# Down projection on unscaled products, with the gate applied at the end and three quadrants added into the output by accumulating DMA

## The chip, the cores and the metric

The kernel runs on one core of a Trainium2 chip. The metric is the device time of one execution in microseconds, as the median of several runs. The core's engines work side by side, each through its own list of instructions in a fixed order: TensorE (PE; its weight loads are listed as PEld), VectorE (DVE), ScalarE (ACT), GpSimd (POOL), and SyncE (SP), which here issues DMA transfers.

## The reference

One block of a diffusion transformer on 1024 tokens of width 1024 (`x`), with 256 context tokens. Only the first layer of the reference is run (`DEPTH = 1`). Cut to what matters:

```python
sh1, sc1, g1, sh2, sc2, g2 = adaln(c, w_mod, b_mod)          # six rows of 1024
h = modulate(rms_norm(x, norm1), sh1, sc1)                   # and the same for the context
y = neighbourhood_attention(q, k, v, kc, vc, rpb) @ w_o      # 16 heads
x = x + g1 * y                                               # called x1 below
h = modulate(rms_norm(x, norm2), sh2, sc2)
a, g = split(h @ w_up, 2)                                    # 2 x 2816 columns
x = x + g2 * ((a * gelu(dwconv_centred(g, conv_w, conv_b))) @ w_down)
```

The last line is the feed-forward part. `g2` is one value for each of the 1024 output columns; `w_down` is 2816 x 1024. Everything is float32.

## The kernel before, in words

Tokens are held in 8 tiles of 128 (`t` = 0 to 7). Every product is taken with operands split into a high part (`h`, a rounded copy made by ScalarE) and a low part (`l`, the rest, a subtraction by VectorE or GpSimd), as three matmuls: high by high, high by low, low by high.

The stages, in the order of the program text: adaLN of the attention branch, attention with the query/key/value projections in between, output projection, second norm (`h2_tile`), up projection with convolution and gate, down projection. The text is only an order of preference: a planner with a cost model of its own lays each engine's instructions out by when it expects them to be ready, preferring those that come earlier in the text. On the chip each engine then keeps to the order laid out, so that an instruction that waits holds up all that stand behind it on its engine. Stages overlap in this way; parts of the down projection stand between parts of the up projection.

`h2_tile(t)` (L621) stores the finished tile of x1 in a scratch tensor `x1_dram`, normalises it and writes the modulated, transposed result over the tile.

The up and the down projection both use a form with seven products of half-size blocks in place of eight. For the down projection the gated rows, and sums of them, were written to `act_dram` by the up projection's `finish`: seven blocks for each of 11 chunks of 256 rows of `w_down`. The chunks are worked in groups of 2, 3, 3 and 3 (`GROUPS`, L45), and in each group the seven products in the order 2, 1, 5, 6, 3, 7, 4 (`DORD`, L58). `seq` lists the 28 pairs (group, product); for each pair there are three steps:

- `prep_b` (L874): on the first pair, and at product 6 of the group before, `load_raw` (L853) fetches the rows of `w_down` as tiles `dr` of 128 x 1024 and multiplies each by `g2b`, the row `g2` on all partitions (L862: of a chunk's two tiles one on GpSimd, the other on VectorE). Products 5, 6, 7 and 4 first form a difference of blocks in place on VectorE (L887 to L893). Then ScalarE makes the high part (L895) and VectorE (products 2, 1, 7) or GpSimd (5, 6, 3, 4) the low part, tile `db` (L896).
- `prep_a` (L865): loads the block of `act_dram` into `da`, and splits it the same way (L869 to L871).
- `down_mm` (L899): for each of four column tiles `j`, nine matmuls (six in the first group) into one of two sets of four PSUM banks, `X` (products 1, 6, 7, 4) and `Y` (2, 5, 3), which go on accumulating over products; then VectorE adds the bank to a half of an accumulator tile `acc[t]` (L914). Each product belongs to one quadrant (row half of the tokens, column half of the outputs): 2 and 1 to (0, 0), 6 and 3 to (0, 1), 5 and 7 to (1, 1), 4 to (1, 0).

`prep_b` runs two pairs ahead of `down_mm`, `prep_a` three. There are 12 buffers for `da` and 10 for `db`. The accumulators are loaded with x1 from `x1_dram` before the first pair (L924), and in the last group, after a quadrant's last product (1, 3, 7, 4), its four tiles are stored to the output by SP (L916). All DMA transfers are issued by SP.

Of the kernel before, what the change touches and what calls it, by code (L numbers as in the profile page):

```python
# [10 lines left out]
F32 = mybir.dt.float32  # L11
F32R = mybir.dt.float32r
AF = mybir.ActivationFunctionType
ALU = mybir.AluOpType
# [4 lines left out]
P = 128  # L19
# [5 lines left out]
NB = 8  # L25
# [11 lines left out]
HALF = 512  # L37
# [7 lines left out]
GROUPS = [2, 3, 3, 3]  # L45
# [8 lines left out]
DG = (1,)  # L54
# [3 lines left out]
DORD = (2, 1, 5, 6, 3, 7, 4)  # L58
# [3 lines left out]
def block_kernel(ctx, tc, x, ctxt, cc, w_mod, b_col, b_row, n1, n2, w_qkv, gains, rpb_t, mask_i, mask_r, w_o,  # L62
                 w_up, conv_w, conv_b, w_down, comb, out):
    nc = tc.nc
    PE, ACT, DVE, POOL, SP = nc.tensor, nc.scalar, nc.vector, nc.gpsimd, nc.sync

    def pool(name, bufs=1, space=None, side=None):
        kw = {}
        if space is not None:
            kw["space"] = space  # L70
        if side is not None:
            kw["side"] = side
        if space is not DRAM:
            kw["reuse_waits"] = "tile"
        return tc.tile_pool(name=name, bufs=bufs, **kw)

    def f(ap):
        return ap.bitcast(F32)

    xv = x.rearrange("(r b j) d -> b r j d", r=ROWS, b=NB, j=8)  # L80
    ov = out.rearrange("(r b j) d -> b r j d", r=ROWS, b=NB, j=8)
# [27 lines left out]
    x1_dram = dram.tile([NB, P, D], F32, name="x1_dram")  # L109
# [5 lines left out]
    def slot(tag, name, dt=F32R, shape=(P, D)):  # L115
        return big.tile(list(shape), dt, tag=tag, bufs=SLOTS[tag], name=name)
# [33 lines left out]
    def norm_rows(t, sq, ss, sqd=False):  # L150
        if sqd:
            DVE.tensor_tensor_reduce(out=sq, in0=t, in1=t, scale=1.0, scalar=0.0, op0=ALU.mult, op1=ALU.add,
                                     accum_out=ss)
        else:
            ACT.activation(sq, t, AF.Square, accum_out=ss)
        DVE.tensor_scalar(ss, ss, 1.0 / D, EPS, ALU.mult, ALU.add)
        POOL.tensor_tensor(ss, ss, mhalf[:, 0:1], ALU.pow)

    # adaLN of the attention branch, normalised and modulated tokens, transposed and split
    att = ExitStack()  # L160
    sa = att.enter_context(pool("sa"))

# [34 lines left out]
    with pool("sm") as sm:  # L197
# [42 lines left out]
        for si in range(4):  # L240
            pm = ps.tile([4, HALF], F32, tag="pq", bufs=2, name=f"pm{si}")
            for k2 in range(4):
                i = 4 * si + k2
# [17 lines left out]
            row = sm.tile([4, HALF], F32, tag="mrow", bufs=1, name=f"mrow{si}")  # L261
# [7 lines left out]
            if si == 3:  # L269
                DVE.tensor_tensor(b1, pc[:, 1], bcol[:, 0:8].unsqueeze(2).broadcast_to([P, KC, 2]), ALU.add)  # L270

    # attention, with the projections of the next pair of heads in between
    sb = att.enter_context(pool("att"))
    mi = sb.tile([P, 3 * P], F32, name="mi")
    SP.dma_start(out=mi, in_=mask_i)
# [179 lines left out]
        DVE.tensor_tensor(res[a:b], po[a:b], tmp[a:b], ALU.add)  # L455
        SP.dma_start(out=o_dram[p, a:b, u * 2 * P:(u + 1) * 2 * P], in_=res[a:b])

    # adaLN of the rest, a little at a time
    def mod_gen():
        order = [2, 3, 4, 5]  # L460
        for sgi in order:
# [27 lines left out]
                        DVE.scalar_tensor_tensor(dst, dst, 1.0, n2c[:, nk * hf:nk * (hf + 1)], ALU.add, ALU.mult)  # L489
                yield  # L490

    # output projection: its first half runs beside the attention of the last heads
    xpool = ctx.enter_context(ExitStack())
    x1, wo, g1b, xsb = {}, [], [], []
    HP = NPAIR // 2
# [79 lines left out]
    for si in range(ns + 4):  # L575
        if si < ns:
            p, h, t = steps[si]
# [7 lines left out]
        if si + 1 < ns and steps[si + 1][2] % 2 == 0:  # L585
            p, h, t = steps[si + 1]
# [6 lines left out]
        if 0 <= si - 3 < ns and steps[si - 3][2] % 2 == 1:  # L593
            p, h, t = steps[si - 3]
# [7 lines left out]
    filler(10 ** 6)  # L602
    att.close()

    # rest of the output projection, second norm, operands of the Winograd form (seven products of halves
    # in place of eight) of the up projection: A is w_up^T in 2 x 2 blocks, B the tokens in 2 x 2 blocks
    ff = ctx.enter_context(ExitStack())
    usb = ff.enter_context(pool("ffn"))
    BT = {}
# [9 lines left out]
                                          name=f"b{op}{hl}{kk}")  # L619

    def h2_tile(t):  # L621
        SP.dma_start(out=x1_dram[t], in_=x1[t])
        xn = slot("wx", f"xn{t}", F32)
        ss = const.tile([P, 1], F32, tag="ss", bufs=3, name=f"ss2{t}")
        norm_rows(x1[t], xn, ss)
        DVE.tensor_scalar(xn, x1[t], ss, None, ALU.mult)
        v = x1[t].rearrange("p (k n) -> p k n", n=P)
        for g in range(2):
            pt = ps.tile([P, 4, P], F32, tag="tr", bufs=3, name=f"pt2{t}_{g}")
            for k in range(4):  # L630
                PE.transpose(pt[:, k, :], xn[:, (4 * g + k) * P:(4 * g + k + 1) * P], ident)
            for k in range(4):
                kk = 4 * g + k
                if g == 0:
                    DVE.tensor_scalar(v[:, kk, :], pt[:, k, :], s2[:, kk:kk + 1], b2[:, kk:kk + 1], ALU.mult, ALU.add)
                else:
                    ACT.activation(v[:, kk, :], pt[:, k, :], AF.Identity, bias=b2[:, kk:kk + 1],
                                   scale=s2[:, kk:kk + 1])
        return v
# [6 lines left out]
            ACT.activation(h, r, AF.Copy)  # L646
            (POOL if op in HP_ else DVE).tensor_tensor(l, r, f(h), ALU.subtract)

    # up projection, gate with the token convolution; the gated rows and their sums go out for the down projection
    NP2 = NF // 2  # L650
    lo_, hi_ = slice(0, HALF), slice(HALF, SEQ)
    uraw, uop = {}, {}
# [161 lines left out]
    for k, (i, part, op) in enumerate(useq):  # L814
# [9 lines left out]
        if op == WORD[-1]:  # L824
# [6 lines left out]
            else:  # L831
                finish(i, y[i])
                if i == 0:
                    g2b = slot("gb", "g2b", F32)
                    SP.dma_start(out=g2b, in_=g_dram[1:2, :].broadcast_to([P, D]))

    # down projection, also in seven products; rows of w_down scaled by the gate g2
    xt = ps.tile([P, 2, HALF], F32, tag="s", bufs=1, name="dx")
    tr = [ps.tile([P, HALF], F32, tag="tr", bufs=3, name=f"dtr{j}") for j in range(3)]
    pq = [ps.tile([P, HALF], F32, tag="pq", bufs=2, name=f"dpq{j}") for j in range(2)]  # L840
# [3 lines left out]
    acc = []  # L844
# [4 lines left out]
    seq = [(n, op) for n in range(len(groups)) for op in DORD]  # L849
# [3 lines left out]
    def load_raw(c):  # L853
        for m in range(2):
            if rt[0] % 14 < 8:
                r = xsb[0].tile([P, D], F32, tag="x1", bufs=NB, name=f"dr{c}_{m}")
            else:
                r = slot("wa", f"dr{c}_{m}", F32)
            rt[0] += 1
            fc = 2 * c + m  # L860
            SP.dma_start(out=r, in_=w_down[fc * P:(fc + 1) * P, :])
            (DVE if m in DG else POOL).tensor_tensor(r, r, g2b, ALU.mult)  # L862
            raws[c, m] = r

    def prep_a(q):  # L865
        n, op = seq[q]
        for c in groups[n]:
            s = usb.tile([P, 2, HALF], F32R, tag="bA", bufs=12, name=f"da{c}_{op}")
            SP.dma_start(out=f(s[:, 1]), in_=act_dram[c, :, AI[op], :])  # L869
            ACT.activation(s[:, 0], f(s[:, 1]), AF.Copy)  # L870
            (DVE if op in DA else POOL).tensor_tensor(s[:, 1], f(s[:, 1]), f(s[:, 0]), ALU.subtract)  # L871
            opa[op, c] = s

    def prep_b(q):  # L874
        n, op = seq[q]
        if q == 0:
            for c in groups[0]:
                load_raw(c)
        if op == RL and n + 1 < len(groups):
            for c in groups[n + 1]:  # L880
                load_raw(c)
        for c in groups[n]:
            s = usb.tile([P, 2, HALF], F32R, tag="bB", bufs=10, name=f"db{c}_{op}")
            r0, r1 = raws[c, 0], raws[c, 1]
            b11, b12, b21, b22 = r0[:, lo_], r0[:, hi_], r1[:, lo_], r1[:, hi_]
            if op == 5:
                DVE.tensor_tensor(b12, b12, b11, ALU.subtract)  # L887
            if op == 6:
                DVE.tensor_tensor(b12, b22, b12, ALU.subtract)
            if op == 7:  # L890
                DVE.tensor_tensor(b22, b12, b11, ALU.subtract)
            if op == 4:
                DVE.tensor_tensor(b21, b21, b12, ALU.subtract)  # L893
            src = {2: b21, 1: b11, 5: b12, 6: b12, 3: b22, 7: b22, 4: b21}[op]
            ACT.activation(s[:, 0], src, AF.Copy)  # L895
            (DVE if op in DB else POOL).tensor_tensor(s[:, 1], src, f(s[:, 0]), ALU.subtract)  # L896
            opb[op, c] = s

    def down_mm(q):  # L899
        n, op = seq[q]  # L900
        start, cs_, bank = op in (2, 1, 5), groups[n], (Y if op in (2, 5, 3) else X)
        row, col = {2: (0, 0), 1: (0, 0), 5: (1, 1), 6: (0, 1), 3: (0, 1), 7: (1, 1), 4: (1, 0)}[op]
        last = n == len(groups) - 1
        for j in range(4):
            o = bank[j]
            for ci, c in enumerate(cs_):
                a, b = opa[op, c], opb[op, c]
                ah, al = (a[:, i, j * P:(j + 1) * P] for i in range(2))
                PE.matmul(o, ah, b[:, 0], start=(start and ci == 0), stop=False, skip_group_check=True)
                PE.matmul(o, ah, b[:, 1], start=False, stop=False, skip_group_check=True)  # L910
                PE.matmul(o, al, b[:, 0], start=False, stop=(ci == len(cs_) - 1), skip_group_check=True)  # L911
            t = j + 4 * row
            d = acc[t][:, col * HALF:(col + 1) * HALF]
            DVE.tensor_tensor(d, o, d, ALU.add)  # L914
            if last and op in (1, 3, 7, 4):
                SP.dma_start(out=ov[t, :, :, col * HALF:(col + 1) * HALF], in_=d)  # L916

    for q in range(LB):
        prep_b(q)
    for q in range(LA):  # L920
        prep_a(q)
    for t in range(NB):
        a_ = slot(("rh", "rl")[t % 2], f"acc{t}", F32)
        SP.dma_start(out=a_, in_=x1_dram[t])  # L924
        acc.append(a_)
    for q in range(len(seq)):
        if q + LB < len(seq):
            prep_b(q + LB)
        if q + LA < len(seq):
            prep_a(q + LA)  # L930
        down_mm(q)


# [46 lines left out]
```

## Time and profile before

| | us |
|---|---|
| median of 3 runs | 1490.04 |
| lowest and highest | 1486.6 and 1491.38 |
| the profiled execution, span from its first to its last instruction | 1491.8 |
| TensorE busy | 1386.5 (93%) |
| VectorE busy | 1208.1 (81%) |
| GpSimd busy | 805.7 (54%) |
| ScalarE busy | 738.1 (49%) |

For the profiled execution the span is the one time given. In the profile's rows a name such as `L862` is a line of the kernel; `out<-in` are tile names; shapes are partitions x elements; `xN` is a count. In rows ordered by time the first number is the start from the beginning of the span, the second the time taken in us; a bracket at the end gives the idle time just before and the instruction that ended it. In rows of groups there stand the busy time in us, the mean of one in ns, and the idle time before them with what ended it. Matmul times overlap, and some of their records can be missing.

### The profile page before, as it was taken

What the parts mean: (1) busy time and instruction counts of PE and PEld (TensorE: products, weight loads), DVE (VectorE), ACT (ScalarE), POOL (GpSimd) and SP (SyncE); (2) the same over time, 40 slices, a digit from 0 to 9 for tenths busy, and PEclk for the clock granted to TensorE, in tenths of its full rate; (3) what the DMA queues carried; (4) which work ended last, traced back from release to release, by engine and by line L of the source; (5) the groups of instructions that cost most, each with busy time, mean ns of one, the idle gap of its engine ahead of it and who ended that gap; (6) DMA issues with size and microseconds to landing.
All of it is one profiled execution on the core that took longest, in us unless ns stands there. A gap on an engine that the chain in (4) does not pass through costs nothing.

```text
span 1491.8 us, 22077 instructions
## 1 busy us (share of the span) xinstructions
PE 1386.5 (93%) x7396; PEld 1200.0 (80%) x7396; DVE 1208.1 (81%) x2392; ACT 738.1 (49%) x1601; POOL 805.7 (54%) x672
## 2 busy tenths in 40 slices
PE   6689999999999999999996999999999987898998
PEld 2589889898989899888885777888888865686887
DVE  6778878888888878866589889788877779988884
ACT  6575645555565656645465434344343334244541
POOL 1455544545454546744368545555545568474872
PEclk9899999999999999999997999999999998899999
DMA  9612221313131202262132132233332347433343
GB/s 315 161 37 60 64 87 55 92 51 103 49 101 45 77 14 73 69 152 76 50 129 99 64 108 101 96 106 106 107 106 99 106 137 286 155 100 127 110 131 105
DMA packets 84827, 153.27 MB, mean 103 GB/s; under 512 B 9945, under 2 KB 49001, under 8 KB 84713
## 3 DMA queue, kind: packets, MB, share of 16 engines
q1 hardware_dynamic: 84712, 151.86, 32.7%
q8 instruction: 58, 0.95, 0.3%
q14 instruction: 57, 0.46, 0.1%
HBM read 119.05 MB, written 32.78 MB: 102 GB/s over the span
## 4 chain that ended last, share of the span: by engine, by line
PE 60%; DVE 20%; DMA 7%; POOL 5%; issue 4%; ACT 3%; SPq 0%; DVEq 0%; POOLq 0%; ACTq 0%
PE pg L740 8%; PE pa L740 7%; PE sw L740 6%; PE pq L301 5%; PE pq L303 5%; PE pq L305 5%; DMA mr<-in_w_mod_dram 2%; DVE y L787 2%; DVE p L410 2%; POOL u L688 2%; PE s L398 2%; PE po L448 2%; PE po L449 2%; PE py L525 2%; PE py L526 2%
## 5 line engine op out<-in xcount | busy, mean ns | idle before, releaser
L688 POOL TENSOR_TENSOR u<-ur,u 128x512 fp32r<-128x512 f32 x154 | 231.9, 1519 | 176.8 <-ACT u L687 175.1
L417 POOL TENSOR_TENSOR p<-p,m 128x640 f32<-128x640 f32 (+1 forms) x128 | 157.3, 1230 | 157.0 <-DVE m L413 116.0
L301 PE MATMUL pq<-wh,hth 128*128 128x384 f32 (+1 forms) x640 | 219.7, 343 | 17.1 <-DVE kn L340 15.3
L305 PE MATMUL pq<-wh,htl 128*128 128x384 f32 (+1 forms) x640 | 215.2, 336 | 2.4 <-DVE htl L194 1.4
L303 PE MATMUL pq<-wl,hth 128*128 128x384 f32 (+1 forms) x640 | 215.0, 336 | 0.5 <-POOL wl L147 0.5
L687 ACT ACTIVATE u<-ur 128x512 fp32r<-128x512 f32 x154 | 93.9, 628 | 116.1 <-PE sw L740 45.4
L412 ACT ACTIVATE p<-p,m 128x640 f32<-128x640 f32 (+1 forms) x128 | 102.9, 804 | 84.3 <-DVE m L410 75.2
L301 PEld LDWEIGHTS pq<-wh,hth 128*128 128x128 f32 x640 | 124.8, 195 | 23.1 <-DVE kn L340 9.2
L325 POOL TENSOR_TENSOR qss<-qss,mhalf 128x4 f32<-128x4 f32 (+1 forms) x80 | 79.9, 999 | 97.0 <-DVE qss L324 82.8
L305 PEld LDWEIGHTS pq<-wh,htl 128*128 128x128 f32 x640 | 124.7, 195 | 3.2 <-DVE htl L194 3.2
L303 PEld LDWEIGHTS pq<-wl,hth 128*128 128x128 f32 x640 | 124.8, 195 | 1.6 <-issue 0.9
L787 DVE SCALAR_TENSOR_TENSOR y<-g,cw,y 128x896 f32<-128x896 f32 (+1 forms) x132 | 102.8, 842 | 19.2 <-ACT y L781 19.1
L449 PE MATMUL po<-pt,v 128*128 128x256 f32 x352 | 93.3, 293 | 2.1 <-DVE pt L437 2.1
L448 PE MATMUL po<-pt,v 128*128 128x256 f32 x352 | 93.8, 289 | 0.1
L895 ACT ACTIVATE db<-dr 128x512 fp32r<-128x512 f32 x77 | 47.4, 629 | 87.3 <-PE dx L911 55.7
L871 POOL TENSOR_TENSOR da<-da 128x512 fp32r<-128x512 f32 x44 | 74.9, 1725 | 27.4 <-ACT da L870 27.4
L896 POOL TENSOR_TENSOR db<-dr,db 128x512 fp32r<-128x512 f32 x44 | 64.9, 1494 | 45.6 <-ACT db L895 34.3
L410 DVE CUSTOM_DVE_ANT_0 p<-s,bias 128x640 f32<-128x640 f32 x96 | 78.3, 816 | 9.5 <-PE s L399 8.9
L436 ACT ACTIVATE pt<-pl 128x384 fp32r<-128x384 f32 (+1 forms) x128 | 58.0, 461 | 47.6 <-PE pl L429 46.6
L471 DVE SCALAR_TENSOR_TENSOR macc<-mr,cs,macc 128x256 f32<-128x256 f32 x112 | 65.0, 581 | 13.9 <-DMA mr<-in_w_mod_dram 13.0
L437 DVE TENSOR_TENSOR pt<-pl,pt 128x384 fp32r<-128x384 f32 (+1 forms) x128 | 65.4, 516 | 6.7 <-ACT pt L436 6.2
L449 PEld LDWEIGHTS po<-pt,v 128*128 128x128 f32 x352 | 66.6, 189 | 4.0 <-DVE pt L437 3.4
(258 smaller groups left out, 4184.3 us busy)
## 6 DMA issues: line engine op xcount, KB each, us to landing
ur<-in_w_up_dram SPq DMA_DIRECT2D x44, 512.0 KB
da<-act_dram SPq DMA_DIRECT2D x77, 256.0 KB
mr<-in_w_mod_dram SPq DMA_DIRECT2D x128, 128.0 KB
dr<-in_w_down_dram SPq DMA_DIRECT2D x22, 512.0 KB
wraw<-in_w_qkv_dram SPq DMA_DIRECT2D x56, 192.0 KB
mraw<-in_w_mod_dram SPq DMA_DIRECT2D x16, 512.0 KB
act_dram<-sa SPq DMA_DIRECT2D x11, 512.0 KB
act_dram<-y SPq DMA_DIRECT2D x11, 512.0 KB
```

The source lines that it names most:

```text
L301: PE.matmul(pq[:, c0:], hth[t][:, k, :], wh[:, c0:], start=(k == 0), stop=False)
L303: PE.matmul(pq[:, c0:], hth[t][:, k, :], wl[:, c0:], start=False, stop=False)
L305: PE.matmul(pq[:, c0:], htl[t][:, k, :], wh[:, c0:], start=False, stop=(k == KC - 1))
L410: DVE.tensor_tensor_reduce(out=dst, in0=src, in1=bb, scale=1.0, scalar=3e38, op0=ALU.add, op1=ALU.min, accum_out=m[:, 0:1])
L412: ACT.activation(w[:, :n], w[:, :n], AF.Exp, bias=m[:, 0:1], scale=-1.0, accum_out=m[:, 1:2])
L417: POOL.tensor_tensor(w[:, :n], w[:, :n], m[:, 2:3].broadcast_to([P, n]), ALU.mult)
L448: PE.matmul(po, v, th[:, j].rearrange("p a b -> p (a b)"), start=(m == 0), stop=False)
L449: PE.matmul(po, v, tl[:, j].rearrange("p a b -> p (a b)"), start=False, stop=(m == len(blks) - 1))
L687: ACT.activation(s[:, 0], r[op], AF.Copy)
L688: POOL.tensor_tensor(s[:, 1], r[op], f(s[:, 0]), ALU.subtract)
L740: PE.matmul(bank, a, b, start=(start and k == 0 and n == 0), stop=(k == 3 and n == 2), skip_group_check=True)
L787: DVE.scalar_tensor_tensor(o, i, w, o, ALU.mult, ALU.add)
```

## The change

`load_raw` no longer multiplies by `g2b`: the matmuls work on `w_down` as it is. The accumulators are no longer loaded with x1, and the products are gated after they are summed.

- In the first group a quadrant's first product (2, 5, 6, 4) is copied to the accumulator by ScalarE in place of the addition on VectorE.
- `h2_tile` stores x1 straight into the output, except for the first column half of tiles 4 to 7 (quadrant (1, 0)), which goes to `x1_dram`.
- In the last group, after the last products of the quadrants (0, 0), (0, 1) and (1, 1), that is after 1, 3 and 7, VectorE adds as before; then the accumulator is multiplied by `g2b` (on VectorE for even `j`, on GpSimd for odd), and GpSimd issues a DMA that adds it to what lies in the output.
- Quadrant (1, 0), whose product 4 is the very last, is gated and joined with x1 by GpSimd after the third group (`PRE`; its x1 is loaded by `load_x1`). At the end VectorE multiplies product 4 of the last group by `g2b` into a scratch tile `gt`, adds it, and SP stores as before.

Comment lines that the diff blanks are left out here.

```diff
     def h2_tile(t):
-        SP.dma_start(out=x1_dram[t], in_=x1[t])
+        if t >= 4:
+            SP.dma_start(out=x1_dram[t, :, :HALF], in_=x1[t][:, :HALF])
+        SP.dma_start(out=ov[t][:, :, HALF * (t >= 4):], in_=x1[t][:, HALF * (t >= 4):])
...
             SP.dma_start(out=r, in_=w_down[fc * P:(fc + 1) * P, :])
-            (DVE if m in DG else POOL).tensor_tensor(r, r, g2b, ALU.mult)
             raws[c, m] = r
...
             t = j + 4 * row
-            d = acc[t][:, col * HALF:(col + 1) * HALF]
-            DVE.tensor_tensor(d, o, d, ALU.add)
-            if last and op in (1, 3, 7, 4):
-                SP.dma_start(out=ov[t, :, :, col * HALF:(col + 1) * HALF], in_=d)
+            c = slice(col * HALF, (col + 1) * HALF)
+            d = acc[t][:, c]
+            if n == 0 and op in (2, 5, 6, 4):
+                ACT.activation(d, o, AF.Copy)
+            elif last and op == DORD[-1]:
+
+                DVE.tensor_tensor(gt[j % 2], o, g2b[:, c], ALU.mult)
+                DVE.tensor_tensor(d, gt[j % 2], d, ALU.add)
+                SP.dma_start(out=ov[t, :, :, c], in_=d)
+            elif last and op in (1, 3, 7):
+
+                DVE.tensor_tensor(d, o, d, ALU.add)
+                (POOL if j % 2 else DVE).tensor_tensor(d, d, g2b[:, c], ALU.mult)
+                POOL.dma_start(out=ov[t, :, :, c], in_=d, accum_op=ALU.add)
+            else:
+                DVE.tensor_tensor(d, o, d, ALU.add)
+            if PRE.get((n, op)) == (row, col):
+                POOL.tensor_tensor(d, d, g2b[:, c], ALU.mult)
+                POOL.tensor_tensor(d, d, x1r[t][:, c], ALU.add)
+
+
+    NG = len(GROUPS) - 1
+    PRE = {(NG - 1, 4): (1, 0)}
+    x1r = {}
+
+    def load_x1():
+        for t in range(4, NB):
+            x1r[t] = slot("wa", f"x1r{t}", F32)
+            SP.dma_start(out=x1r[t][:, lo_], in_=x1_dram[t, :, lo_])
...
     for t in range(NB):
-        a_ = slot(("rh", "rl")[t % 2], f"acc{t}", F32)
-        SP.dma_start(out=a_, in_=x1_dram[t])
-        acc.append(a_)
+        acc.append(slot(("rh", "rl")[t % 2], f"acc{t}", F32))
+    g_ = slot("r4", "gt", F32, (P, 2, HALF))
+    gt = [g_[:, i] for i in range(2)]
     for q in range(len(seq)):
...
+        if seq[q] == (NG - 1, DORD[-1]):
+            load_x1()
         down_mm(q)
```

## The prediction

> **What bounds the kernel now.** I read the page first, then the busy time by stretches of the last 300 us, the waits of TensorE, and the order in time of VectorE, GpSimd and the DMA queue there.
>
> ```profile
> span 1491.8 us, 22077 instructions
> 1000.00:1100.00 100.00, 100.00 (x431) 80.76 (x430) 82.16 (x98) 39.15 (x61) 51.22 (x36) 1.00 0.32 108
> 1200.00:1242.50 42.50, 36.89 (x156) 28.48 (x154) 34.09 (x39) 17.25 (x28) 24.89 (x15) 1.00 0.54 187
> 1242.50:1300.00 57.50, 44.40 (x160) 33.97 (x160) 55.63 (x57) 16.68 (x29) 42.72 (x20) 0.85 0.62 221
> 1300.00:1346.00 46.00, 46.00 (x204) 37.68 (x203) 40.77 (x51) 18.17 (x30) 29.09 (x19) 1.00 0.37 116
> 1346.00:1364.00 18.00, 12.45 (x46) 9.16 (x45) 14.14 (x19) 8.79 (x15) 11.87 (x7) 0.91 0.44 142
> 1422.00:1487.50 65.50, 65.21 (x288) 53.68 (x286) 40.90 (x51) 19.74 (x32) 35.09 (x24) 1.00 0.41 118
> ```
>
> The columns are the stretch, its length, then busy time and count of PE, PEld, DVE, ACT, POOL, the granted clock, DMA share and GB/s. In the up projection TensorE is never idle (100.00 of 100). It loses time where the up projection hands over to the down projection, and once more near 1350. At full clock a matmul takes 46.00/204 = 0.2255 us. The stretch 1242.5 to 1300 has 160 of them, 36.1 us of work in 57.5: 21.4 us are lost, and there VectorE is busy 55.63 of 57.5, so VectorE bounds it. 1200 to 1242.5 loses 42.50 - 36.89 = 5.6, and 1346 to 1364 loses 18.0 - 46 x 0.2255 = 7.6. Together 34.6 us can be had here, and no more. After 1364 TensorE bounds again.
>
> ```profile
> PE dpq L909 <- DVE acc L914: 4.8, 2, 4.0
> PE dpq L909 <- DVE tmp L762: 4.3, 1, 4.3
> PE pg L740 <- ACT tmp L772: 3.2, 1, 3.2
> PE dx L909 <- DVE acc L914: 5.4, 2, 4.7
> 1210.59 1.23 DVE L862 TENSOR_TENSOR dr<-dr,g2b 128x1024 f32<-128x1024 f32 x1 [1.29 <-DMA dr<-in_w_down_dram]
> 1265.30 8.34 POOL L862 TENSOR_TENSOR dr<-dr,g2b 128x1024 f32<-128x1024 f32 x3
> 1266.41 2.25 DVE L804 TENSOR_TENSOR sa<-y,y 128x512 f32<-128x512 f32 x1
> 1268.58 2.85 DVE L806 TENSOR_TENSOR sb<-y 128x512 f32<-128x512 f32 x1
> 1271.36 2.82 DVE L766 TENSOR_TENSOR y<-tmp,y 128x512 f32<-128x512 f32 x1
> 1274.11 0.68 DVE L914 TENSOR_TENSOR acc<-dpq,acc 128x512 f32<-128x512 f32 x1
> 1274.71 0.68 DVE L805 TENSOR_TENSOR sa<-sa,y 128x512 f32<-128x512 f32 x1
> 1288.36 3.41 DVE L862 TENSOR_TENSOR dr<-dr,g2b 128x1024 f32<-128x1024 f32 x1
> 1294.68 2.38 DVE L887 TENSOR_TENSOR dr<-dr 128x512 f32<-128x512 f32 x1
> 1354.07 2.35 POOL L862 TENSOR_TENSOR dr<-dr,g2b 128x1024 f32<-128x1024 f32 x1 [0.86 <-DMA dr<-in_w_down_dram]
> 1356.45 1.73 DVE L887 TENSOR_TENSOR dr<-dr 128x512 f32<-128x512 f32 x1 [3.86 <-POOL dr L862]
> ```
>
> The first four rows say what TensorE waited for (us in total, times, longest): an evacuation that VectorE had not reached. The rest (start, us) shows why. A VectorE operation with both inputs in SBUF takes 0.68 us alone (1274.71) and 2.25 to 2.85 while GpSimd multiplies dr by g2b (1265.30 to 1273.64); behind them in VectorE's order stood the evacuation at 1274.11 that ended TensorE's 4.0 us wait.
>
> **The change, part by part.**
>
> ```profile
> L862 POOL TENSOR_TENSOR dr<-dr,g2b 128x1024 f32<-128x1024 f32 x10 | 25.7, 2582 | 13.7 <-DMA dr<-in_w_down_dram 13.7
> L862 DVE TENSOR_TENSOR dr<-dr,g2b 128x1024 f32<-128x1024 f32 x10 | 15.4, 1544 | 1.3 <-DMA dr<-in_w_down_dram 1.3
> L914 DVE TENSOR_TENSOR acc<-dtr,acc 128x512 f32<-128x512 f32 x48 | 32.1, 680 | 9.6 <-PE dtr L911 9.6
> L772 ACT ACTIVATE tmp<-pa 128x512 f32<-128x512 f32 x5 | 2.7, 582 | 0.0
> 1240.00:1250.00 10.00, 7.14 (x24) 5.09 (x23) 8.76 (x13) 7.85 (x15) 9.30 (x3) 0.83 1.02 397
> acc<-x_dram SPq DMA_DIRECT2D x8, 512.0 KB
> ```
>
> *Gating of w_down, removed.* 22 multiplications go, 11 on each engine (20 fall after 1195). *First evacuations, moved.* 16 additions of group 0, 0.60 us each at back-to-back pace (1274.11 to 1274.71), become copies on ScalarE, 0.58 each by L772's row, 9.3 us in all; ScalarE is busy 16.68 of 57.5 there, which covers it. *Loads of acc, removed.* 4.2 MB leave the DMA engines, full in 1240 to 1250 (share 1.02).
>
> In 1242.5 to 1300 VectorE is rid of five multiplications (four of about 1.2 and the 3.41 one: 8.2 us), of 9.6 us of additions, and of the stretching of four operations by GpSimd's multiplications (2.25 + 2.85 + 2.82 + 2.38 - 4 x 0.68 = 7.6): 25.4 of its 55.63, which leaves 30 beside the 36.1 that TensorE needs. VectorE stops being the bound. What stays late is the tail of the last convolution and the contention with GpSimd's subtractions, which nothing removes: I leave 6.4 of the 21.4 there and take 15. In the first stretch the wait of 1.29 for a load and its multiplication of 1.23 go from VectorE's order, and they stood ahead of ScalarE's late copy (the 3.2 us wait): 4.5 of 5.6. Near 1350 the 2.35 on GpSimd goes, but VectorE then waits for that load directly (it was at most 3.86 idle there): half of 7.6, 3.8. Sum: 23.3 gained.
>
> ```profile
> L622 SPq DMA_DIRECT2D x_dram<-x x8: 327/332/333, 740.5 to 792.4; - x8
> L916 SPq DMA_DIRECT2D out_dram<-acc x16: 538/539/597, 1441.1 to 1488.0; - x16
> 1424.72 1.73 POOL L896 TENSOR_TENSOR db<-dr,db 128x512 fp32r<-128x512 f32 x1 [10.45 <-ACT db L895]
> 1456.24 1.30 POOL L896 TENSOR_TENSOR db<-dr,db 128x512 fp32r<-128x512 f32 x1 [4.91 <-ACT db L895]
> L871 POOL TENSOR_TENSOR da<-da 128x512 fp32r<-128x512 f32 x12 | 18.8, 1594 | 0.0
> L896 POOL TENSOR_TENSOR db<-dr,db 128x512 fp32r<-128x512 f32 x12 | 16.6, 1402 | 15.4 <-ACT db L895 15.4
> 1240.70 8.61 POOL L871 TENSOR_TENSOR da<-da 128x512 fp32r<-128x512 f32 x2 [6.38 <-ACT da L870]
> 1487.25 0.69 DVE L914 TENSOR_TENSOR acc<-dx,acc 128x512 f32<-128x512 f32 x1 [1.35 <-PE dx L911]
> 18.95 0.56 POOL L157 TENSOR_TENSOR ss<-ss,mhalf 128x1 f32<-128x1 f32 x1 [17.61 <-DVE ss L156]
> 41.87 0.55 POOL L157 TENSOR_TENSOR ss<-ss,mhalf 128x1 f32<-128x1 f32 x1 [1.34 <-DVE ss L156]
> ```
>
> *Stores of x1, split in h2_tile.* Four more issues on SP, 0.33 us each; no wait in the trace ends on these stores, so nothing. If that cover failed, 1.3 us.
>
> *Gate and x1 on one quadrant after group 2 (PRE), and gates plus accumulating DMAs in the last group: GpSimd's new load.* An operation of a three-chunk group is 36 matmuls of 65.21/288 = 0.2264: 8.15 us. Back from TensorE's end at 1487.2, the last group starts at 1430.1 and its op 3 (the fifth) at 1462.7. GpSimd has from 1424.7 to there 38.0 us. Its 18 subtractions for ops 5, 6 and 3 take 26.6 at the mean of the two groups (35.4/24 = 1.48); before, it had gaps of 10.45 and 4.91 here. New are 8 PRE operations (11.8), two gates of op 1 (3.0) and four DMA issues of c each: 41.4 + 4c, or 3.4 + 4c too long. What waits for GpSimd is op 3's db, and TensorE behind it.
>
> No row shows a DMA issued by GpSimd. c lies between SP's 0.54 for the same store (L916) and 4.3, the slowest GpSimd operation of this size (1240.70, 8.61 for two). It is nearer to the issue than to an elementwise pass, so I take 1.0. Then op 3 is 7.4 late, and the slow clock after such a gap costs 2 more (1346 to 1364: 12.45 busy for 10.4 of work): 9.4. If the planner sets op 1's gates and DMAs behind op 3's subtractions, 0.4 is left. Program order speaks two to one for the first: 6.4.
>
> The Trainium skill's "SBUF — State Buffer", section "SBUF: two separate sides" (the "DVE blocks DMA" trap), says that a GpSimd DMA of 0.62 us became about 3.1 us beside a VectorE copy that held the shared ports. Under "Who interferes with whom" it takes tensor_tensor out of that, by inference; with c = 3.1 the formula below ends at 1498.9, with 0.62 at 1472.
>
> *x1r, four loads of 256 KB.* They stand on SP behind da loads that wait for TensorE; PRE's addition may wait some 2 to 4 us for them (a store of that size lands 3.9 after its data: 1491.8 less 1487.94). It is inside the 6.4's spread. *VectorE's gates of ops 1, 3, 7* (6 x 0.68): it is busy 40.90 of 65.5 there, nothing. *The end.* Op 4's last tile needs a multiplication and an addition where it needed one: +0.6, then the same 3.9 for the store. *Last accumulating DMAs.* After op 3's db, GpSimd has 6 subtractions, 4 gates and 8 issues, 14.8 + 8c, then 3.9 to land; TensorE has 3 x 8.15 and 5.2 of ending: 8c - 11 is exposed, below zero at c = 1.0, so nothing.
>
> Sum: -23.3 + 6.4 + 0.6 = -16.3, a span of 1475.5. The profiled span is 1.8 above the median of the runs (1490.0), so I forecast 1474.
>
> **The rivals.**
> 1. *Nothing given back*: the planner fits GpSimd's new work into its gaps of 10.45 and 4.91. For it: GpSimd is busy 35.09 of 65.5. Against: the gaps lie beside deadlines, and the work comes in bursts. -23.3 + 0.6: 1467.
> 2. *Slower: the GpSimd-issued DMA is dear.* Loss is 3.4 + 4c + 2 + 0.6, plus 8c - 11 at the end; it eats the 23.3 at c = 2.4, and passes 0.3% slower at 2.73. At 4.3 it is 46.6: 1513. Between, some 1504. For it: the 4.3 row. Against: the issue moves no data through the engine.
> 3. *The handover does not loosen*: VectorE waits for loads and GpSimd's subtractions as it did for the multiplications, and only the waits that the rows tie to them go: 1.29 + 1.23, 4.0, 2.35, together 8.9. Less 6.4 and 0.6, 1.9 remain: 1488. For it: the 4.3 us wait on L762 names no multiplication.
> 4. *A pause at the first DMA of GpSimd.* The first use of an operation shows none (0.56 at 18.95, 0.55 at 41.87), so by rows it is 0 to the 2.58 of its longest group: up to 1477. The Trainium skill's "GPSIMD Engine Reference", section 2.1 Instruction dispatch, has the first call of freshly loaded code pay about 6 us; that would end at 1480, and the two rows do not show it.
>
> **How the numbers follow.** The forecast 0.45, rival 1 0.20, rival 2 0.14, rival 3 0.14, rival 4 0.07. A measurement can tell 0.3%, 4.5 us: faster (forecast, 1 and 4) 0.72, same (3) 0.14, slower (2) 0.14. The likeliest case alone spans 1468 (give-back 0.4) to 1482 (4 us less at the handover and 4 more given back). The range leaves out rival 2 and a few below rival 1, where all 34.6 went: 1462 to 1492.
>
> **What would show it.** TensorE's busy share in the 57 us of the handover rises from 0.77 to over 0.9, with VectorE under 0.7; no acc loads, and ScalarE copies into acc. In the last group TensorE waits once, some 5 to 10 us, for GpSimd's db at op 3, and GpSimd has no gaps there. The span ends on op 4's plain store. Wrong: GpSimd's issues above 2.4 us, an end set by an accumulating DMA, or VectorE still full at the handover.

## The result, and the profile after

The changed kernel takes 1476.24 us (median of 4 runs, 1472.09 to 1477.30) against 1489.55 for the kernel before (4 runs, 1486.60 to 1491.38). The ratio is 0.9903, 95% interval 0.9887 to 0.9918: about 1.0% faster. The profiled execution has a span of 1474.2 us; its own time is 1475.98, so 1.8 us lie around a span. By the same 1.8 the profiled execution of the kernel before (span 1491.8) took some 1493.6, about 4 above its median, while that of the changed kernel lies at its median: the spans differ by 17.6, the medians by 13.3.

The stretches of the end in the changed kernel, with the columns as before (stretch, length, busy time and count of PE, PEld, DVE, ACT, POOL, clock, DMA share, GB/s):

```profile
span 1474.2 us, 22076 instructions
1200.00:1242.50 42.50, 36.53 (x152) 28.48 (x151) 34.78 (x40) 21.20 (x35) 23.02 (x16) 0.94 0.51 179
1242.50:1300.00 57.50, 55.58 (x240) 45.16 (x240) 44.79 (x60) 26.73 (x46) 21.97 (x17) 0.99 0.50 180
1300.00:1346.00 46.00, 46.00 (x205) 38.09 (x204) 37.38 (x50) 23.61 (x38) 27.63 (x20) 1.00 0.51 164
...
1346.00:1364.00 18.00, 18.00 (x81) 14.92 (x80) 14.86 (x16) 8.93 (x16) 18.00 (x13) 1.00 0.28 89
1404.00:1475.00 71.00, 58.67 (x247) 47.42 (x245) 54.57 (x51) 13.75 (x23) 55.95 (x45) 0.94 0.49 98
```

From 1200 to 1364 TensorE now does 152 + 240 + 205 + 81 = 678 matmuls where it did 156 + 160 + 204 + 46 = 566: 112 more, 25.3 us of work at 0.2255. In 1242.5 to 1300 VectorE fell from 55.63 us busy to 44.79 and TensorE rose from 44.40 to 55.58. The last row is the other side: up to TensorE's end at 1468.6 it lost 64.6 - 247 x 0.2255 = 8.9 us, in a part where it had lost almost nothing. Of these, 5.9 are idle (58.67 busy in 64.6); the other 3.0 are matmuls that took longer, at a granted clock of 0.94 in that row.

What TensorE waited for from 1190 on (us in total, times, longest), and then GpSimd, VectorE and TensorE in order of time at the later of the two long waits:

```profile
PE dpo L911 <- DVE db L897: 5.6, 1, 5.6
PE dx L910 <- DVE acc L929: 5.5, 1, 5.5
PE dx L910 <- DVE tmp L764: 1.9, 1, 1.9
PE dpq L911 <- POOL db L897: 0.4, 1, 0.4
```

```profile
1431.62 1.03 POOL L927 DMA_DIRECT2D out_dram<-acc  x1
1432.38 1.60 POOL L926 TENSOR_TENSOR acc<-acc,g2b 128x512 f32<-128x512 f32 x1
1433.63 1.59 POOL L897 TENSOR_TENSOR db<-dr,db 128x512 fp32r<-128x512 f32 x1
1434.86 1.16 POOL L927 DMA_DIRECT2D out_dram<-acc  x1
1435.44 1.89 POOL L897 TENSOR_TENSOR db<-dr,db 128x512 fp32r<-128x512 f32 x1
1436.69 1.87 POOL L926 TENSOR_TENSOR acc<-acc,g2b 128x512 f32<-128x512 f32 x1
1437.93 1.88 POOL L872 TENSOR_TENSOR da<-da 128x512 fp32r<-128x512 f32 x1
1439.16 1.46 POOL L927 DMA_DIRECT2D out_dram<-acc  x1
1439.73 3.41 POOL L872 TENSOR_TENSOR da<-da 128x512 fp32r<-128x512 f32 x2
1442.22 1.70 POOL L927 DMA_DIRECT2D out_dram<-acc  x1
...
1435.25 8.45 DVE L892 TENSOR_TENSOR dr<-dr 128x512 f32<-128x512 f32 x1 [2.93 <-POOL db L897]
1443.62 0.68 DVE L929 TENSOR_TENSOR acc<-dtr,acc 128x512 f32<-128x512 f32 x1
...
1447.00 0.68 DVE L929 TENSOR_TENSOR acc<-dx,acc 128x512 f32<-128x512 f32 x1
...
1447.73 0.80 PE L910 MATMUL dx<-db,da 128*128 128x512 f32 x1 [5.53 <-DVE acc L929]
```

GpSimd works here without a break (an elementwise operation starts some 1.2 us before the next instruction, and the rows overlap). One VectorE difference of two SBUF blocks (product 7's), 0.68 us alone, takes 8.45 beside it; it had already waited 2.93 for GpSimd's db. Six operations behind it, at 1447.00, VectorE evacuates product 6's `dx`, and this is what ends TensorE's wait. This is the main part of the give-back, and it came about on VectorE: TensorE waited for GpSimd's db itself only 0.4 us.

The matmul that waited writes product 3's half of `dx`. The two halves of this one tile serve the bank sets `X` and `Y`, and the evacuation that ended the wait is of the other half. Whether two separate tiles would have spared the wait, no run shows.

The end, and GpSimd's DMAs (the first two lines are VectorE's last; then the group of issues with its mean; then the transfer, with the median us from issue to landing):

```profile
1468.61 0.69 DVE L920 TENSOR_TENSOR gt<-dx,g2b 128x512 f32<-128x512 f32 x1 [0.62 <-PE dx L912]
1469.33 0.69 DVE L921 TENSOR_TENSOR acc<-gt,acc 128x512 f32<-128x512 f32 x1
...
L927 POOL DMA_DIRECT2D out_dram<-acc x12 | 12.7, 1124 | 1.8 <-DVE acc L926 1.7
...
out_dram<-acc POOLq DMA_DIRECT2D x12, 256.0 KB, 4.3
```

From TensorE's end to the end of the span it is now 1474.2 - 1468.6 = 5.6, before 4.5: 1.1 longer. The last accumulating DMA is issued by 1464.7 and does not set the end. One part of the 17.6 us between the two spans is not shown to be the change's: it lies ahead of the up projection's first matmul.

```profile
L740 PE MATMUL pa<-b1h,u x88: 395/396/792, 795.7 to 1231.1; 128*128 128x512 f32 x88
...
L742 PE MATMUL pa<-b1h,u x88: 395/396/795, 793.7 to 1223.0; 128*128 128x512 f32 x88
```

It starts at 795.7 before and 793.7 after. In the runs below it starts between 789.7 and 797.1, in kernels that up to there differ from one of these two by a store at most, so a difference of a few us between the spans of two single profiles says nothing; the medians with their intervals do.

### The profile page after: what moved, and what is told of

The parts are those of the page before. It is cut to its first block, busy times and chain, and to the rows that moved or that the text cites. A ratio compares the mean times of both kernels' runs of the same rounds, so it can differ in the third digit from the quotient of the medians.

```text
span 1474.2 us, 22076 instructions
## 1 busy us (share of the span) xinstructions
PE 1380.1 (94%) x7396; PEld 1197.4 (81%) x7396; DVE 1188.2 (81%) x2375; ACT 746.5 (51%) x1617; POOL 793.0 (54%) x687
## 5 line engine op out<-in xcount | busy, mean ns | idle before, releaser
L690 POOL TENSOR_TENSOR u<-ur,u 128x512 fp32r<-128x512 f32 x154 | 227.6, 1491 | 192.1 <-ACT u L689 191.6
L872 POOL TENSOR_TENSOR da<-da 128x512 fp32r<-128x512 f32 x44 | 67.9, 1592 | 29.5 <-PE dtr L912 17.4
```

Of the source, the lines that this page charges most:

```text
L690: POOL.tensor_tensor(s[:, 1], r[op], f(s[:, 0]), ALU.subtract)
```

## The experiments

Two questions: what made the handover faster, and what was given back in the last group. Theory V: VectorE's queue, relieved of multiplications (its own, and GpSimd's, which stretch its operations) and of 16 evacuations. Theory D: 4.2 MB of loads less on full DMA engines. For the last group, theory G: GpSimd has too many operations; theory N: its DMA issues among them hold VectorE up. "After" is the changed kernel.

| run | median us | ratio to before, 95% interval |
|---|---|---|
| after | 1476.2 | 0.9903 (0.9887 to 0.9918) |
| mult_back | 1498.6 | 1.0049 (1.0031 to 1.0067) |
| load_back | 1475.7 | 0.9906 (0.9884 to 0.9928) |
| vector_copy | 1475.9 | 0.9902 (0.9883 to 0.9922) |
| no_mult_only | 1467.9 | 0.9840 (0.9813 to 0.9868) |
| no_pre | 1469.3 | 0.9847 (0.9820 to 0.9874) |
| plain_store | 1469.6 | 0.9856 (0.9831 to 0.9881) |
| gate_vector | 1473.6 | 0.9874 (0.9853 to 0.9895) |
| pool_plain | 1472.4 | 0.9883 (0.9860 to 0.9907) |
| all_add | 1471.8 | 0.9860 (0.9835 to 0.9885) |
| all_add_gates | 1468.3 | 0.9858 (0.9832 to 0.9884) |
| all_add_first | 1466.9 | 0.9840 (0.9821 to 0.9860) |
| all_add_both | 1468.2 | 0.9848 (0.9833 to 0.9864) |

The medians of the kernel before were 1489.6 beside after and 1490.2 to 1491.4 beside the rest; each ratio is to the runs of before taken with it.

### The multiplications put back (mult_back)

```diff
             SP.dma_start(out=r, in_=w_down[fc * P:(fc + 1) * P, :])
+            (DVE if m in DG else POOL).tensor_tensor(r, r, g2b, ALU.mult)
             raws[c, m] = r
```

> The changed kernel with the 22 multiplications of w_down's rows by g2 put back as they were (the output is gated twice). Theory V (the handover got faster because VectorE's queue was relieved of its own and GpSimd's multiplications and of 16 evacuations): most of the gain goes again, 10 to 16 us slower than the changed kernel, some 1486 to 1492, and TensorE's busy share in the handover falls back towards 0.8. Theory D (it got faster because 4.2 MB of accumulator loads left full DMA engines): at most 3 us slower, 1476 to 1479.

1498.6, that is 22.3 us slower than after: more than theory V's 10 to 16. Most of what the handover had gained went: from 1200 to 1364 TensorE does 587 matmuls by the four stretches, against 678 in after and 566 before, so some 5 us stay (near 1350, 74 matmuls for 46). With what the last group costs the kernel is slower than before. The stretch 1242.5 to 1300 of this run:

```profile
1242.50:1300.00 57.50, 43.75 (x155) 32.78 (x155) 51.67 (x49) 22.91 (x42) 44.13 (x21) 0.85 0.49 163
```

It is nearly the row of before again: 155 matmuls (160), clock 0.85, GpSimd at 44.13 (42.72), though loads and evacuations stayed moved.

### The accumulator loads put back (load_back)

```diff
     for t in range(NB):
-        acc.append(slot(("rh", "rl")[t % 2], f"acc{t}", F32))
+        a_ = slot(("rh", "rl")[t % 2], f"acc{t}", F32)
+        SP.dma_start(out=a_, in_=xv[t])
+        acc.append(a_)
```

> The changed kernel with eight loads of 512 KB into the accumulators put back at their old place (from the input x, and overwritten by the first copies, so that only their traffic and their place in the DMA queue remain). Theory V: 0 to 3 us slower than the changed kernel, 1476 to 1479. Theory D: 8 us or more slower, 1484 and above, with da and dr landing later in the handover.

1475.7, no slower than after. Theory D falls: it asked for 8 us or more, and the interval leaves some 4 at most. TensorE's waits did move (the one of 5.6 for `db` shrank to 0.9, and new ones of 1.0 and 2.8 came), but from 1200 to 1364 it does 676 matmuls, as good as the 678 of after.

### The first evacuations on VectorE (vector_copy)

```diff
-                ACT.activation(d, o, AF.Copy)
+                DVE.tensor_copy(d, o)
```

> The changed kernel with the 16 first evacuations of group 0 as copies on VectorE in place of ScalarE. Theory V: VectorE has 13 us to spare in the 57.5 us of the handover and gets 9.6 back, so 2 to 5 us slower, 1478 to 1481. Theory D: no difference, 1475 to 1477.

1475.9, no slower either, where theory V expected 2 to 5 us; the interval leaves room for some 3. The stretch 1242.5 to 1300:

```profile
1242.50:1300.00 57.50, 56.30 (x239) 45.39 (x238) 49.56 (x74) 17.38 (x28) 18.23 (x15) 0.97 0.50 174
```

Once the multiplications are gone VectorE has room for 16 evacuations (49.56 of 57.5, with TensorE at 56.30); with them gone, moving the evacuations brought nothing that can be measured.

### The multiplications taken out of the kernel before, and nothing else (no_mult_only)

```diff
             SP.dma_start(out=r, in_=w_down[fc * P:(fc + 1) * P, :])
-            (DVE if m in DG else POOL).tensor_tensor(r, r, g2b, ALU.mult)
             raws[c, m] = r
```

> The kernel before without the 22 multiplications, and nothing else changed (its feed-forward part is not gated). Theory V: the multiplications alone bring 12 to 18 of the 23.3 us of the handover, and nothing is given back in the last group: 1472 to 1478. Theory D: 1486 to 1490, as before.

1467.9 against 1491.4: 23.5 us (by the ratio's interval some 20 to 28), below the expected range of times, and as much as the handover gained in all. Accumulator loads and VectorE's evacuations are all there. TensorE's largest waits in it:

```profile
PE dtr L908 <- DVE acc L913: 3.1, 1, 3.1
PE dpq L908 <- DVE tmp L762: 2.8, 1, 2.8
```

So theory V holds in its part on the multiplications alone. Which of them did it, VectorE's own eleven or GpSimd's eleven that stretch VectorE's operations, no run separates. Against this run the changed kernel is some 8 to 9 us slower (1476.2 to 1467.9 by the medians, 0.9903 to 0.9840 by the ratios); by mult_back against before it is 7.2 (1498.6 to 1491.4), less the some 5 us that mult_back kept in the handover. So the two pairs of kernels, one without and one with the multiplications, agree only roughly on the price for gating at the end.

### Without the operations after the third group (no_pre)

```diff
-    PRE = {(NG - 1, 4): (1, 0)}
+    PRE = {}
...
-        if seq[q] == (NG - 1, DORD[-1]):
-            load_x1()
```

> The changed kernel without the eight GpSimd operations that gate quadrant (1, 0) and add x1 to it after the third group, and without x1's four loads (that quadrant lacks x1 and the gate on three groups). Theory G (the 5.5 us gap and the slow clock in the last group come from GpSimd's load, the eight operations being 11 of its some 60 us there): the gap goes, 6 to 8 us faster than the changed kernel, 1468 to 1470. Theory N (the gap comes from the DMA issues: the VectorE difference of 8.45 us at 1435 stood behind five GpSimd operations and two issues that ran without a break): the long difference stays, at most 3 us faster, 1473 or above.

1469.3: theory G's number. The 5.5 us wait is gone (0.2 left). But the long VectorE operation is not; it moved ahead to one that nothing urgent stood behind:

```profile
1418.51 6.39 DVE L897 TENSOR_TENSOR db<-dr,db 128x512 fp32r<-128x512 f32 x1
```

### Plain stores by SP (plain_store)

```diff
-                POOL.dma_start(out=ov[t, :, :, c], in_=d, accum_op=ALU.add)
+                SP.dma_start(out=ov[t, :, :, c], in_=d)
```

> The changed kernel with the twelve accumulating DMAs of GpSimd as plain stores by SP (the output lacks x1 in three quadrants). Theory G: GpSimd still has the eight operations and the gates, the gap shrinks by the four issues of product 1, some 4 us: 1471 to 1474. Theory N: no difference on VectorE takes over 4 us, the gap goes, 6 to 8 us faster: 1468 to 1470. If accumulating DMAs cost nothing, 1475 to 1477.

1469.6: theory N's number, with GpSimd's eight operations and its gates all in place. The same difference of product 7 as in after, and GpSimd around it:

```profile
1434.38 2.54 POOL L897 TENSOR_TENSOR db<-dr,db 128x512 fp32r<-128x512 f32 x2
1436.86 1.77 POOL L926 TENSOR_TENSOR acc<-acc,g2b 128x512 f32<-128x512 f32 x1
...
1435.71 1.77 DVE L892 TENSOR_TENSOR dr<-dr 128x512 f32<-128x512 f32 x1 [2.49 <-POOL db L897]
```

1.77 in place of 8.45, with a wait of 2.49 before it (2.93 in after). No VectorE operation of the last group takes over 1.78 us. So each theory has half: the eight operations make GpSimd late, so that this difference becomes urgent; the issues make VectorE wait behind GpSimd's whole run. Take either away and the gap goes. The issues also took GpSimd's time, and this run takes away both that and their place among its operations.

### GpSimd issues plain DMAs (pool_plain)

```diff
-                POOL.dma_start(out=ov[t, :, :, c], in_=d, accum_op=ALU.add)
+                POOL.dma_start(out=ov[t, :, :, c], in_=d)
```

> The changed kernel with its twelve GpSimd DMAs left in place and on GpSimd, but plain: they overwrite the output and add nothing (three quadrants lack x1). If what holds VectorE up is that GpSimd issues DMAs between its own operations, the long VectorE difference (8.45 us) and TensorE's gap (5.5 us) stay: 1474 to 1478. If it is the adding in the DMA engines, they go as they did with plain stores by SP: 1468 to 1471.

1472.4, between the two, and the interval overlaps that of after and that of plain_store: the time decides nothing here, and the trace has to. The adding made an issue longer (median 0.55 us here, 1.15 in after), but without it VectorE was held as well:

```profile
1431.94 5.05 DVE L892 TENSOR_TENSOR dr<-dr 128x512 f32<-128x512 f32 x1 [2.62 <-POOL db L897]
...
PE dx L910 <- DVE acc L929: 3.8, 1, 3.8
```

So the adding is not needed for the hold: GpSimd's issues between its own operations are enough. That the adding makes it longer (8.45 to 5.05) is read from one trace of this run.

### All gates on VectorE (gate_vector)

```diff
-                (POOL if j % 2 else DVE).tensor_tensor(d, d, g2b[:, c], ALU.mult)
+                DVE.tensor_tensor(d, d, g2b[:, c], ALU.mult)
```

> The changed kernel with all twelve gates of products 1, 3 and 7 on VectorE (six were on GpSimd). Theory G: GpSimd loses 2 operations (3 us) ahead of product 3's subtractions, the gap shrinks by about 3 us: 1472 to 1474. Theory N: fewer GpSimd operations to stand behind but the same issues, 0 to 2 us faster. Against both: VectorE gets six more operations that contend with GpSimd.

1473.6, as theory G had it: TensorE's wait is 3.2 in place of 5.5, the difference takes 4.74. The intervals (0.9853 to 0.9895, after 0.9887 to 0.9918) overlap a little.

### All four quadrants by accumulating DMA (all_add)

```diff
     def h2_tile(t):
-        if t >= 4:
-            SP.dma_start(out=x1_dram[t, :, :HALF], in_=x1[t][:, :HALF])
-        SP.dma_start(out=ov[t][:, :, HALF * (t >= 4):], in_=x1[t][:, HALF * (t >= 4):])
+        SP.dma_start(out=ov[t], in_=x1[t])
...
-            elif last and op == DORD[-1]:
-
-                DVE.tensor_tensor(gt[j % 2], o, g2b[:, c], ALU.mult)
-                DVE.tensor_tensor(d, gt[j % 2], d, ALU.add)
-                SP.dma_start(out=ov[t, :, :, c], in_=d)
-            elif last and op in (1, 3, 7):
+            elif last and op in (1, 3, 7, 4):
...
-                (POOL if j % 2 else DVE).tensor_tensor(d, d, g2b[:, c], ALU.mult)
+                (POOL if j % 2 and op != 4 else DVE).tensor_tensor(d, d, g2b[:, c], ALU.mult)
...
-    PRE = {(NG - 1, 4): (1, 0)}
+    PRE = {}
...
-        if seq[q] == (NG - 1, DORD[-1]):
-            load_x1()
```

> The changed kernel with the fourth quadrant treated like the others: no operations after the third group, no x1 loads, x1 whole in the output, and product 4 of the last group added by VectorE, gated by VectorE and added to the output by four more accumulating DMAs. Theory G: the gap goes as in the run without the eight operations, and the end is 1 to 2 us longer (an accumulating DMA lands 4.3 us after its issue, the issue takes 1.1, against 3.9 for a plain store): 1469 to 1472. Theory N: the gap stays and the end is longer: 1475 to 1478.

1471.8, in theory G's range, and faster than after, if by little: its interval ends at 0.9885, that of after begins at 0.9887. It computes the whole block, with less code. In the profiled execution, the fastest of the five, TensorE does not wait in the last group; the long operation (6.38) is there, off the path.

### Two edits of that version (all_add_gates, all_add_first, all_add_both)

All gates on VectorE (`DVE.tensor_tensor(d, d, g2b[:, c], ALU.mult)`, all_add_gates):

> The version with all four quadrants added by accumulating DMA, with all gates on VectorE: GpSimd has no operation of its own between the issues but the subtractions. If a VectorE operation with two SBUF inputs has to wait until GpSimd's run of operations and issues ends, the longest one falls from 6.4 to 3 to 5 us. TensorE has no gap in the last group to lose, so the time stays: 1470 to 1473; at best 1 us less.

1468.3, a little below the expected range; the longest held operation fell from 6.38 to 2.65, also below what was expected, and the interval of the ratio is that of all_add, so the time is no better than all_add's as far as this shows.

Four subtractions of the first group on GpSimd (all_add_first):

```diff
-            (DVE if op in DB else POOL).tensor_tensor(s[:, 1], src, f(s[:, 0]), ALU.subtract)
+            (DVE if n and op in DB or not n and op == 7 else POOL).tensor_tensor(s[:, 1], src, f(s[:, 0]), ALU.subtract)
```

> The version with all four quadrants added by accumulating DMA, with the low parts of w_down for products 2 and 1 of the first group on GpSimd in place of VectorE: four subtractions. The one wait of TensorE left in the handover (5.5 us) ends on such a subtraction, which VectorE reaches late. If it is VectorE's queue that is late, the wait shrinks by 2 to 5 us: 1466 to 1470. If it is the port shared with GpSimd's six subtractions just before, GpSimd's queue is now the late one and nothing is won: 1471 to 1475.

1466.9, the lowest median. TensorE's wait of 5.5 is gone from its place, and another came:

```profile
PE pa L740 <- ACT tmp L772: 3.3, 1, 3.3
PE dtr L908 <- DVE acc L922: 1.6, 1, 1.6
```

Both together (all_add_both):

> The version with all four quadrants added by accumulating DMA, with both small edits: the four subtractions of the first group on GpSimd, and all gates on VectorE. The first edit took the wait of 5.5 us out of the handover, the second shortened a VectorE wait that was not on the path. If that reading holds, this is as fast as the first edit alone: 1465 to 1468. If the gates' place matters for the time, 2 us or more faster than that.

1468.2. These four cannot be told apart by their intervals (0.982 to 0.989). All four lie below the changed kernel's, all_add and all_add_gates by a hair, and each is faster than both kernels of this case. That the first group's edit brings anything beyond all_add is not shown.

## Why the prediction was right or wrong, point by point

The forecast was 1474; measured were 1476.2, inside the likeliest case's own range of 1468 to 1482. A span of 1475.5 was forecast and 1474.2 seen, 2.0 us of it won ahead of the up projection. By the medians the kernel was to win 16 us and won 13.3. The mechanism was right in the handover and half right in the last group. That the sum came so close is in part luck: by the stretches the handover won 25.3 where 23.3 was forecast, the last group gave back 8.9 for 6.4 and the end 1.1 for 0.6, and errors inside the first of these cancelled too.

- *VectorE bounds the handover, and the multiplications are what to take from it*: right. 23.3 was forecast for the whole change; the multiplications alone brought 23.5 (20 to 28 by the interval).
- *How the 23.3 is made up*: its parts did not come out. The relief of VectorE was put at 25.4 us, 9.6 of them evacuations; moving those is worth nothing that can be measured (vector_copy). VectorE was to be left with 30 of the 57.5 us, under 0.7 of the stretch; it is busy 44.79, 0.78. The prediction held VectorE's work in the stretch at what it had been, but TensorE does 240 matmuls there in place of 160, and VectorE's work for them comes along. It is enough that VectorE no longer fills the stretch (50.95 in no_mult_only, 49.56 in vector_copy, 44.79 in after); below that, less VectorE time bought nothing measurable. The other error was of the opposite sign: 6.4 of 21.4 were left as lost in 1242.5 to 1300 and 3.8 of 7.6 near 1350. In after about 3 are left in the one (57.5 - 240 x 0.2255 = 3.4) and nothing in the other. In exchange the first stretch, where 4.5 of 5.6 were to be won, lost as much as before (the 5.6 counts idle time only; by the count of matmuls it was 42.5 - 156 x 0.2255 = 7.3, and is 8.2 in after). The wait of 3.2 us on ScalarE went as forecast, but one of 5.6 came at 1235 to 1240, behind VectorE operations stretched by GpSimd's six subtractions. The prediction had named such contention as what stays, for the next stretch:

```profile
1230.44 9.43 POOL L872 TENSOR_TENSOR da<-da 128x512 fp32r<-128x512 f32 x6 [10.34 <-ACT da L871]
...
1232.23 4.84 DVE L789 SCALAR_TENSOR_TENSOR y<-g,cw,y 128x112 f32<-128x112 f32 x3
1238.67 3.43 DVE L897 TENSOR_TENSOR db<-dr,db 128x512 fp32r<-128x512 f32 x2
```

- *The loads of acc*: counted at nothing beyond the relief of the DMA engines, and worth nothing that can be measured.
- *The give-back in the last group*: forecast 6.4, weighed between 9.4 and 0.4 by the planner's order; 8.9 by the trace of after. Together with the end 7.0 was forecast, and no_mult_only against after gives 8 to 9. The order was the first of the two: product 1's gates and issues stand among and ahead of product 3's subtractions. The place of the wait was only half right. TensorE was to wait for GpSimd's db; it waited for an evacuation on VectorE, six operations behind one that was held beside GpSimd. The step that failed is this wait: the prediction priced GpSimd's new work by GpSimd's own time and VectorE's new work at nothing, and had no term for what GpSimd's run does to VectorE: one operation of 0.68 us that took 8.45.
- *c, the price of an accumulating DMA's issue*: taken as 1.0 between 0.54 and 4.3; 1.12 on average. Rival 2 needed 2.4. The 4.3 was the mean of two operations in one row, of 1.6 and 7.05, not the slowest one. And with c = 0.62 the formula of rival 2 ends at 1475, not at 1472.
- *The end*: +0.6 forecast, 1.1 measured; the last store landed 0.3 later after its data than before. *The landing* of an accumulating DMA: 3.9 taken, 4.3 measured, hidden.
- *A pause at GpSimd's first DMA* (rival 4): none; the first issue took 1.03 us (the row at 1431.62), no more than the rest. The 6 us of the Trainium skill's "GPSIMD Engine Reference", section 2.1 Instruction dispatch, do not show here; whether an issue counts as such code, no run shows.
- *Nothing given back* (rival 1) is what no_pre and plain_store come near, each by leaving out a part of the work: 1469.3 and 1469.6, where 1467 was given.

## What to carry to other kernels

When an engine bounds a stretch, take away the work that other engines wait behind in its order, and stop when it no longer fills the stretch: the multiplications were worth 23.5 us, and moving the evacuations as well nothing that could be measured. An operation moved to the end has to be priced in the stretch where it lands, on every engine that the new work can hold up, since the queue that is late there need not be the one that got the work. GpSimd issuing DMAs between its own elementwise operations is dear for VectorE (8.45 us for one operation in after); with the gates moved to VectorE the longest hold was 4.74 (gate_vector), with the eight operations after the third group gone as well 2.65 (all_add_gates), and with plain stores by SP there was none (1.78 at most).

## What the runs showed of the hardware that was not expected

A VectorE operation with two SBUF inputs beside GpSimd's elementwise operations took at most 1.78 us in the last group as long as GpSimd issued no DMA (plain_store: its 0.68 and the rest of one GpSimd operation). With issues among GpSimd's operations one was held over several of them: 8.45 us in after and 6.39 in no_pre, until GpSimd's elementwise operations ran out; 4.74 in gate_vector and 5.05 with plain DMAs, where GpSimd still had subtractions to do when it was let go; 2.65 in all_add_gates. The Trainium skill's "SBUF — State Buffer", section "Who interferes with whom", has the second to issue blocked until the first finishes, for the whole instruction; plain_store agrees (1.77), and the 8.45, over five of GpSimd's operations and two issues, does not. Why VectorE was not let in between there, no run shows.

Nor do the runs show that only issues bring such a hold. The kernel before, where GpSimd issues no DMA, has one the other way round: of the two GpSimd subtractions in the prediction's row at 1240.70, one took 7.05 us, from 1242.27 to 1249.32, where 1.3 is usual alone. VectorE was then doing one operation with two SBUF inputs after another, and GpSimd's ended 1.2 us after VectorE came to one with an input in PSUM (`sw`):

```profile
1245.67 2.49 DVE L896 TENSOR_TENSOR db<-dr,db 128x512 fp32r<-128x512 f32 x4
1248.08 0.68 DVE L774 TENSOR_TENSOR tmp<-sw,tmp 128x512 f32<-128x512 f32 x1
```

GpSimd's issues were not held up by VectorE in this way: they took 0.82 to 1.70 us in after.
